# Sample-token products of a hybrid decoder step: the states move through TensorE, and padded k and q columns are the weights

## Chip, core and metric

The kernel runs on one core of one Trainium2 chip. The metric is the device time of one execution in microseconds. TensorE does the matrix products, VectorE (DVE), ScalarE (ACT) and GpSimd (POOL) do the elementwise work, and SyncE (SP) issues most of the transfers.

## What is computed

One layer of a decoder is applied to 512 prompt tokens and to 8 sample tokens. The mixer is a gated delta rule with 8 heads of width 128 beside a pooling group, followed by an output projection and a SwiGLU network. The change concerns the sample tokens alone. For each of the 8 sequences `b` and each of the 8 heads `h` there is a state, a 128 x 128 matrix S, and the recurrent step needs two vectors out of it:

```python
def gated_delta_recurrent(q, k, v, g, beta, S0):
    def step(S, xs):
        q_t, k_t, v_t, g_t, b_t = xs
        S = S * jnp.exp(g_t)[..., None, None]
        kv = jnp.einsum('bhk,bhkv->bhv', k_t, S)
        S = S + jnp.einsum('bhk,bhv->bhkv', k_t, (v_t - kv) * b_t[..., None])
        o = jnp.einsum('bhk,bhkv->bhv', q_t, S)
        return S, o
```

With one token the output can be had from the products of k and q with the incoming state, so the kernel computes k·S and q·S for all 64 pairs (h, b) and does the rest on vectors. The updated states are written much later, in the feed-forward part, from the same inputs.

## The kernel before

**Staging.** The kernel holds the normalised input as two parts `xh` and `xl` of 16 tiles of 128 x 520 (8 sample columns and 512 prompt columns). Every weight granule is loaded as `raw` (L131), cut into `hi` on ScalarE (L135) and `lo` on VectorE (L137), and each product is made of three passes (L168 to L170). One column tile of the input projection is a call of `product`: 16 steps over the depth for the first chunk of columns, and the same for the second chunk three steps behind it.

**The weave.** Small work of the delta rule is written as Python generators and put on tracks of a `Weave`. `product` calls `weave.step()` 16 times for a tile, and each call lets the first task of each track run until its next `yield n`, after which that track rests for n steps. TensorE's instructions are issued in exactly this written order; for the other engines a scheduler orders them by readiness and priority. So a step of the weave is the unit in which small TensorE work is spread between large matmuls.

**The stage of the change.** After the last head's delta rule the pooling tiles run (`pool_tile` for t = 6, 7, 4, 5, 2, 3, 0, 1). Woven into them, on track 0, are `conv_out`, `sample_norms`, eight calls of `sample_product` and `sample_out`; on track 1 is `pool_mix`. After them come the subtraction of L203 over the mixer's first half (`mixa`, its sample columns included, which `sample_out` writes in its L1015) and the splits of the mixer's tiles into `xh` and `xl` (`split`, L194 and L195), which the output projection (L1176 to L1178) reads.

**`sample_norms`** forms k and q of the sample tokens in `kqs`, a tile of 128 x (head, sequence, 2), with k in place 0 and q in place 1 of the last axis. It yields 8, then forms the norms.

**`sample_product(h)`** loads the eight states of a head as two tiles of four (`s0`, L983, through SP's queue, two buffers under the tag `uu`). For each state it issues one f32 matmul with the state as the 128 x 128 weights and the two columns of `kqs` as the moving operand (L986), and yields one step after each. The result is two columns of a PSUM bank. After eight states VectorE copies 16 columns into `smp["kq"]` (L988). A bank comes from `pst()`, which has five.

**`sample_out`** is the chain of vector operations on `kq` (L998 to L1007), a rest of four steps, a matmul with ones (L1010), an inverse root (`rsqrt_wide`) and the write into `mixa` (L1015); it also turns the update vectors and stores them (L1018 to L1021).

**`utfs`** are two tiles of 128 x 1024 that hold the blocks of the triangular inverses for even and odd heads. `delta` reads them (L860, L864, L870, L872), and they are not used after the last head.

Of the kernel before, what the change touches and what calls it, by code (L numbers as in the profile page):

```python
# [17 lines left out]
P = 128  # L18
# [5 lines left out]
H = 8  # L24
# [45 lines left out]
def decoder_kernel(ctx, tc, x_prompt, x_sample, state_delta, state_conv, state_pool, norm_mix, w_in,  # L70
# [4 lines left out]
    te, act, dve, pool, sp = nc.tensor, nc.scalar, nc.vector, nc.gpsimd, nc.sync  # L75
# [12 lines left out]
    def pst():  # L88
        return ps_dn.tile([P, 512], F32, tag="dn", name="dn")


    ident = const.tile([P, P], F32, name="ident")
# [124 lines left out]
    def rsqrt_wide(r, v, t):  # L217

        act.activation(t, v, AF.Sqrt)
        dve.reciprocal(r, t)  # L220
        dve.tensor_tensor(t, v, r, op=ALU.mult)
        dve.tensor_tensor(t, t, r, op=ALU.mult)
        dve.tensor_scalar(t, t, -0.5, 1.5, op0=ALU.mult, op1=ALU.add)
        dve.tensor_tensor(r, r, t, op=ALU.mult)
# [52 lines left out]
    with tc.tile_pool(name="ph0", bufs=2) as ph0, tc.high_priority(offset=10 * AHEAD), tc.manual_schedule():  # L277
# [112 lines left out]
        half = slice(0, D // 2), slice(D // 2, D)  # L390
# [49 lines left out]
        for i in range(17):  # L440
# [48 lines left out]
            ci, j = divmod(i, 8)  # L489
# [31 lines left out]
    with ExitStack() as p1:  # L521
# [4 lines left out]
        def d1tile(tag, shape, name, dtype=F32):  # L526
            return (pre if tag == "ext" else d1).tile(shape, dtype, tag=tag, name=name, bufs=BUFS[tag])

        def scratch(*tags):

            width = {"nb": 1024, "u": 1024}
            tiles = [[d1tile(t, [P, width.get(t, SEQ)], "sc_" + t), 0] for t in tags]

            def take(n):
                for x in tiles:
                    if x[1] + n <= x[0].shape[1]:
                        x[1] += n
                        return x[0][:, x[1] - n:x[1]]
                raise ValueError(n)

            return take
# [99 lines left out]
        kqs = gt.tile([P, H, NB, 2], F32, name="kqs")  # L641
# [69 lines left out]
        utfs = []  # L711
        for i in range(2):
            ut = gt.tile([P, 2, NCH, P], F32, name=f"utf{i}")
# [234 lines left out]
        smp = {}  # L948

        def sample_norms():  # L950
            take = scratch("nb", "u")
            smp["take"] = take
            ys = take(192).rearrange("p (t b) -> p t b", t=24)
            dve.tensor_tensor(ys, ccs.rearrange("p b t -> p t b"),
                              prm[:, 72:96].rearrange("p (t o) -> p t o", o=1).broadcast_to([P, 24, NB]), op=ALU.mult)
            dve.tensor_tensor(ys, ys, scv, op=ALU.add)
            act.activation(kqs[:, :, :, 1], ys[:, 0:8, :], AF.Silu)
            act.activation(kqs[:, :, :, 0], ys[:, 8:16, :], AF.Silu)
            act.activation(vsm, ys[:, 16:24, :], AF.Silu)
            kk, qq = kqs[:, :, :, 0], kqs[:, :, :, 1]  # L960
            sq = take(192).rearrange("p (a h b) -> p a h b", a=3, h=H)
            pool.tensor_tensor(sq[:, 0], kk, kk, op=ALU.mult)
            pool.tensor_tensor(sq[:, 1], qq, qq, op=ALU.mult)
            pool.tensor_tensor(sq[:, 2], kk, qq, op=ALU.mult)
            yield 8
            pn = pst()
            te.matmul(pn[:, 0:192], ones, sq.rearrange("p a h b -> p (a h b)"), start=True, stop=True)
            nv = take(128)
            dve.tensor_scalar(nv, pn[:, 0:128], EPS, None, op0=ALU.add)
            kqd = take(HB)  # L970
            dve.tensor_copy(kqd, pn[:, 128:192])
            rn = take(128)
            rsqrt_wide(rn, nv, take(128))
            smp["rk"], smp["rq"], smp["kqd"] = rn[:, 0:64], rn[:, 64:128], kqd
            dve.tensor_tensor(kns, kk, rn[:, 0:64].rearrange("p (h b) -> p h b", h=H), op=ALU.mult)
            smp["kq"] = take(2 * HB)

        def sample_product(h):

            pk = pst()  # L980
            for hf in range(2):
                s0 = d1tile("uu", [P, 4, P], "s0")
                sp.dma_start(s0, state_delta[0, 4 * hf:4 * hf + 4, h].rearrange("b k v -> k b v"))  # L983
                for j in range(4):
                    b = 4 * hf + j
                    te.matmul(pk[:, 2 * b:2 * b + 2], s0[:, j, :], kqs[:, h, b, :], start=True, stop=True)  # L986
                    yield 1
            dve.tensor_copy(smp["kq"][:, 16 * h:16 * h + 16], pk[:, 0:16])  # L988

        def sample_out():  # L990
            take = smp["take"]
            rk, rq, kqd = smp["rk"], smp["rq"], smp["kqd"]
            pkv = smp["kq"].rearrange("p (n j) -> p n j", j=2)
            vv = vsm.rearrange("p h b -> p (h b)")
            ks, qs, t1, us = take(HB), take(HB), take(HB), take(HB)
            eg = sgb[:, 0].rearrange("p h b -> p (h b)")
            be = sgb[:, 1].rearrange("p h b -> p (h b)")
            dve.tensor_tensor(t1, eg, rk, op=ALU.mult)  # L998
            dve.tensor_tensor(ks, pkv[:, :, 0], t1, op=ALU.mult)
            dve.tensor_tensor(qs, pkv[:, :, 1], eg, op=ALU.mult)  # L1000
            dve.tensor_tensor(us, vv, ks, op=ALU.subtract)
            dve.tensor_tensor(us, us, be, op=ALU.mult)
            dve.tensor_tensor(t1, kqd, rk, op=ALU.mult)
            dve.tensor_tensor(t1, t1, us, op=ALU.mult)
            dve.tensor_tensor(qs, qs, t1, op=ALU.add)
            dve.scalar_tensor_tensor(qs, qs, float(P) ** -0.5, rq, op0=ALU.mult, op1=ALU.mult)
            dve.tensor_tensor(t1, qs, qs, op=ALU.mult)  # L1007
            yield 4
            po = pst()
            te.matmul(po[:, 0:HB], ones, t1, start=True, stop=True)  # L1010
            ov, ro = take(HB), take(HB)
            dve.tensor_scalar(ov, po[:, 0:HB], 1.0 / P, EPS, op0=ALU.mult, op1=ALU.add)
            rsqrt_wide(ro, ov, take(HB))
            dve.tensor_tensor(ro, ro, qs, op=ALU.mult)
            dve.scalar_tensor_tensor(mixa[:, :, 0:NB], ro.rearrange("p (h b) -> p h b", h=H), dnw, mixa[:, :, 0:NB],  # L1015
                                     op0=ALU.mult, op1=ALU.mult)
            pu = pst()
            te.transpose(pu[:HB, 0:P], us, ident)  # L1018
            ur = take(P)[:HB]
            dve.tensor_copy(ur, pu[:HB, 0:P])  # L1020
            sp.dma_start(u_d, ur)  # L1021
            yield 1
# [105 lines left out]
        for b in range(2):  # L1128
# [10 lines left out]
            for h in range(4 * b, 4 * b + 4):  # L1139
                qv_tiles(h)  # L1140
        weave.add(conv_out())
        weave.add(sample_norms())
        for h in range(H):
            weave.add(sample_product(h))
        weave.add(sample_out())
        splits = {}

# [105 lines left out]
    class Pair:  # L1253
# [31 lines left out]
        def take(self):  # L1285
            return pst()[:, :HALF]
# [771 lines left out]
    pt = pst()  # L2058
# [45 lines left out]
```

## Time and profile before

| what | value |
|---|---|
| median of 3 runs | 2156.06 us (2155.36 to 2157.12) |
| the profiled execution, own time | 2156.18 us |
| its span on the core | 2154.4 us |
| granted TensorE clock | 1.0 throughout |
| first and last product (L986) start | 515.2 and 581.0 us |
| states loaded for the products | 16 transfers of 256 KB |

The span runs from the first to the last instruction; the execution's own time is 1.8 us longer. In the rows of the profile, `PE` is a matmul on TensorE and `PEld` its weight load, which overlaps the matmul before it. A row `128*32 128x264` means 128 rows by 32 columns of weights, and 264 moving columns. The lengths of matmuls contain the way through the array and overlap one another, so the price of an instruction in a full stream is read from the distance of starts, not from its length.

### The profile page before, as it was taken

What the parts mean: (1) busy time and instruction counts of PE and PEld (TensorE: products, weight loads), DVE (VectorE), ACT (ScalarE), POOL (GpSimd) and SP (SyncE); (2) the same over time, 40 slices, a digit from 0 to 9 for tenths busy, and PEclk for the clock granted to TensorE, in tenths of its full rate; (3) what the DMA queues carried; (4) which work ended last, traced back from release to release, by engine and by line L of the source; (5) the groups of instructions that cost most, each with busy time, mean ns of one, the idle gap of its engine ahead of it and who ended that gap; (6) DMA issues with size and microseconds to landing.
All of it is one profiled execution on the core that took longest, in us unless ns stands there. A gap on an engine that the chain in (4) does not pass through costs nothing.

```text
span 2154.4 us, 43035 instructions
## 1 busy us (share of the span) xinstructions
PE 2129.6 (99%) x17745; PEld 2121.1 (98%) x17745; DVE 1759.6 (82%) x2635; ACT 929.0 (43%) x1404; POOL 481.9 (22%) x592
## 2 busy tenths in 40 slices
PE   8999999999999999999999999999999999999998
PEld 7999999999999999999999999999999999999998
DVE  7786767666599979888888888888887897887997
ACT  6533452433255454434434434434334444435444
POOL 2112320231012202333233233232113302003100
PEclk9999999999999999999999999999999999999999
DMA  8344434443445534454455455454456746438333
GB/s 282 92 121 110 116 103 117 115 117 98 128 126 166 152 105 124 144 170 144 137 172 147 134 172 147 134 172 133 118 148 195 228 111 205 115 104 247 93 108 119
DMA packets 445826, 305.44 MB, mean 142 GB/s; under 512 B 27836, under 2 KB 424533, under 8 KB 442285
## 3 DMA queue, kind: packets, MB, share of 16 engines
q1 hardware_dynamic: 422733, 219.94, 36.5%
q0 software_dynamic: 21584, 81.95, 12.0%
q8 instruction: 139, 2.28, 0.4%
q10 hardware_dynamic: 1312, 0.80, 0.1%
q14 instruction: 58, 0.48, 0.1%
HBM read 255.66 MB, written 47.63 MB: 141 GB/s over the span
## 4 chain that ended last, share of the span: by engine, by line
PE 85%; DVE 8%; DMA 2%; ACT 2%; issue 2%; POOL 1%; DVEq 0%; ACTq 0%; POOLq 0%; SPq 0%
PE dn L1250 21%; PE dn L1249 21%; PE dn L1251 21%; PE mm L168 6%; PE mm L170 5%; PE mm L169 5%; DVE lo L1243 1%; DVE lo L137 1%; PE dn L870 1%; DMA st<-a_d 1%; DVE raw L1271 1%; POOL st L1803 0%; DVE tm L836 0%; PE dn L986 0%; DVE u L838 0%
## 5 line engine op out<-in xcount | busy, mean ns | idle before, releaser
L1243 DVE TENSOR_TENSOR lo<-raw,hi 128x1024 fp32r<-128x1024 f32 (+1 forms) x422 | 528.6, 1272 | 89.5 <-ACT hi L1242 87.4
L1242 ACT CAST hi<-raw 128x1024 fp32r<-128x1024 f32 (+1 forms) x422 | 427.5, 1027 | 402.9 <-DVE raw L1271 204.2
L168 PE MATMUL mm<-xh,hi 128*128 128x256 f32 (+1 forms) x1280 | 379.5, 297 | 2.6 <-DVE mixa L259 2.6
L169 PE MATMUL mm<-xl,hi 128*128 128x256 f32 (+1 forms) x1280 | 361.6, 283 | 0.9 <-DVE xl L350 0.5
L170 PE MATMUL mm<-xh,lo 128*128 128x256 f32 (+1 forms) x1280 | 361.7, 283 | 0.4 <-DVE lo L137 0.4
L168 PEld LDWEIGHTS mm<-xh,hi 128*128 128x128 f32 x1280 | 241.4, 189 | 3.8 <-DVE mixa L259 3.2
L169 PEld LDWEIGHTS mm<-xl,hi 128*128 128x128 f32 x1280 | 241.7, 189 | 1.7 <-DVE xl L350 1.7
L170 PEld LDWEIGHTS mm<-xh,lo 128*128 128x128 f32 x1280 | 240.9, 188 | 0.6 <-DVE lo L137 0.6
L1271 DVE TENSOR_TENSOR raw<-raw 128x1024 f32<-128x1024 f32 (+1 forms) x130 | 174.6, 1343 | 2.2
L1250 PE MATMUL dn<-b21l,hi 128*128 128x260 f32 x620 | 175.8, 284 | 0.4 <-DVE b21l L1813 0.4
L1251 PE MATMUL dn<-b21h,lo 128*128 128x260 f32 x620 | 175.4, 283 | 0.0
L1249 PE MATMUL dn<-b21h,hi 128*128 128x260 f32 x620 | 174.9, 282 | 0.0
L1251 PE MATMUL dn<-b11h,lo 128*128 128x260 f32 x612 | 173.2, 283 | 1.4 <-DVE lo L1243 1.4
L1250 PE MATMUL dn<-b11l,hi 128*128 128x260 f32 x612 | 173.3, 283 | 0.0
L1249 PE MATMUL dn<-b11h,hi 128*128 128x260 f32 x612 | 172.7, 282 | 0.0
L1435 POOL TENSOR_TENSOR mixa<-mixa 128x520 f32<-128x520 f32 x22 | 51.3, 2330 | 495.5 <-DVE mixa L1429 495.5
L1249 PE MATMUL dn<-T1h,hi 128*128 128x260 f32 x556 | 158.1, 284 | 0.0
L1250 PE MATMUL dn<-T1l,hi 128*128 128x260 f32 x556 | 157.7, 284 | 0.0
L1251 PE MATMUL dn<-T1h,lo 128*128 128x260 f32 x556 | 156.7, 282 | 0.0
L1249 PE MATMUL dn<-B22h,hi 128*128 128x260 f32 x548 | 155.9, 284 | 0.0
L1250 PE MATMUL dn<-B22l,hi 128*128 128x260 f32 x548 | 155.6, 284 | 0.0
L1251 PE MATMUL dn<-B22h,lo 128*128 128x260 f32 x548 | 154.6, 282 | 0.4 <-DVE lo L1243 0.4
(663 smaller groups left out, 6504.0 us busy)
## 6 DMA issues: line engine op xcount, KB each, us to landing
raw<-in_w_gate_up_dram SPq DMA_DIRECT2D x134, 512.0 KB
raw<-in_w_in_dram SPq DMA_DIRECT2D x79, 512.0 KB
a_d<-mixa POOLq DMA_DIRECT2D x22, 1040.0 KB, 5.5
raw<-in_w_down_dram SPq DMA_DIRECT2D x48, 448.0 KB
mixb<-in_w_gate_up_dram SPq DMA_DIRECT2D x41, 512.0 KB
raw<-in_w_out_dram SPq DMA_DIRECT2D x25, 512.0 KB
st<-a_d POOLq DMA_DIRECT2D x49, 260.0 KB, 6.8
raw<-in_w_down_dram SPq DMA_DIRECT2D x24, 512.0 KB
```

What stands on the lines that cost most here:

```text
L137: dve.tensor_tensor(lo[:, r], raw[:, r], hi[:, r].bitcast(F32), op=ALU.subtract)
L168: te.matmul(acc[ci], wh, hi[k][:, c0:c1], start=(k == 0), stop=False)
L169: te.matmul(acc[ci], wh, lo[k][:, c0:c1], start=False, stop=False)
L170: te.matmul(acc[ci], wl, hi[k][:, c0:c1], start=False, stop=(k == len(w) - 1))
L870: te.matmul(yp[0:96, c, j], xt_[:, c, :], udf[:, c, j] if it == 0 else v3(cur)[:, c, j], start=True, stop=True)
L1242: act.copy(hi, raw)
L1243: dve.tensor_tensor(lo, raw, hi.bitcast(F32), op=ALU.subtract)
L1249: te.matmul(acc, wh[:, k, :], xf[:, k, :], start=start and k == 0, stop=False)
L1250: te.matmul(acc, wh[:, k, :], xg[:, k, :], start=False, stop=False)
L1251: te.matmul(acc, wl[:, k, :], xf[:, k, :], start=False, stop=stop and k == wh.shape[1] - 1)
L1271: dve.tensor_tensor(r[name], r[a], r[b], op=op)
L1435: pool.tensor_tensor(q[:, 4:8:2, :], q[:, 1:4:2, :], q[:, 0:2, :], op=ALU.subtract)
```

## The change

The roles of state and vector are exchanged. The states become the moving operand (128 columns), and k and q become weights. For this `sample_norms` builds four areas of 512 columns in the two `utfs` tiles, which are free by then: each is cleared on POOL, and k and q of the 16 states with the same j = b mod 4 are copied in on a diagonal, so that the block of 32 columns with number i holds k and q of its state in columns 2i and 2i + 1 and zeros elsewhere. Four states of one load, j = 0 to 3, then use four groups of 32 columns: the j-th writes the PSUM rows 32j to 32j + 31. All 16 loads add up in the same 128 x 128 block of PSUM: the zeros keep the other rows as they are. The four matmuls of a load are issued together, followed by a rest of four steps, in place of one matmul in each of four steps.

The eight copies out of PSUM go. In their place `sample_out` first copies the block, rests two steps, turns it on TensorE and copies the result into `kq` in the order (i, j, t) that the rest expects.

```diff
@@ -974,22 +974,41 @@
             smp["kq"] = take(2 * HB)
+            smp["cols"] = []
+            kqf = kqs.rearrange("p h b t -> p (h b) t")
+            for ut in utfs:
+                uf = ut.rearrange("p a c j -> p (a c j)")
+                pool.memset(uf, 0.0)
+                for half in range(2):
+                    j, z = len(smp["cols"]), uf[:, 512 * half:512 * half + 512]
+                    src = kqf[:, j:2 * H * 4:4, :]
+                    pool.tensor_copy(z[:, 0:510].rearrange("p (i x) -> p i x", x=34)[:, :, 0:2], src[:, 0:15, :])
+                    pool.tensor_copy(z[:, 510:512], src[:, 15, :])
+                    smp["cols"].append(z)
 
         def sample_product(h):
 
-            pk = pst()
+            if h == 0:
+                smp["pk"] = pst()
             for hf in range(2):
                 s0 = d1tile("uu", [P, 4, P], "s0")
                 sp.dma_start(s0, state_delta[0, 4 * hf:4 * hf + 4, h].rearrange("b k v -> k b v"))
+                i = 2 * h + hf
                 for j in range(4):
-                    b = 4 * hf + j
-                    te.matmul(pk[:, 2 * b:2 * b + 2], s0[:, j, :], kqs[:, h, b, :], start=True, stop=True)
-                    yield 1
-            dve.tensor_copy(smp["kq"][:, 16 * h:16 * h + 16], pk[:, 0:16])
+                    te.matmul(smp["pk"][32 * j:32 * j + 32, 0:P], smp["cols"][j][:, 32 * i:32 * i + 32], s0[:, j, :],
+                              start=(i == 0), stop=(i == 2 * H - 1))
+                yield 4
 
         def sample_out():
             take = smp["take"]
             rk, rq, kqd = smp["rk"], smp["rq"], smp["kqd"]
+            kt = take(P)
+            dve.tensor_copy(kt, smp["pk"][:, 0:P])
+            yield 2
+            pt = pst()
+            te.transpose(pt[:, 0:P], kt, ident)
+            dve.tensor_copy(smp["kq"].rearrange("p (i j t) -> p j i t", j=4, t=2),
+                            pt[:, 0:P].rearrange("p (j i t) -> p j i t", j=4, t=2))
             pkv = smp["kq"].rearrange("p (n j) -> p n j", j=2)
```

## The prediction

> **What bounds the kernel now.** I read the page's busy times first, then its chain of work that ended last, then busy times by stretches around the sample products.
>
> ```profile
> span 2154.4 us, 43035 instructions
> PE 2129.6 (99%) x17745; PEld 2121.1 (98%) x17745; DVE 1759.6 (82%) x2635; ACT 929.0 (43%) x1404; POOL 481.9 (22%) x592
> ...
> PE 85%; DVE 8%; DMA 2%; ACT 2%; issue 2%; POOL 1%; DVEq 0%; ACTq 0%; POOLq 0%; SPq 0%
> ```
> ```profile
> 565.00:581.50 16.50, 16.49 (x139) 16.29 (x140) 7.29 (x17) 2.92 (x4) 0.43 (x3) 1.00 0.52 144
> 581.50:600.00 18.50, 18.50 (x157) 18.50 (x156) 16.10 (x40) 10.73 (x18) 0.21 (x1) 1.00 0.32 89
> 600.00:620.00 20.00, 19.65 (x162) 19.24 (x161) 18.64 (x33) 10.57 (x19) 1.93 (x1) 1.00 0.29 79
> 620.00:640.00 20.00, 19.77 (x164) 19.44 (x162) 19.70 (x31) 11.37 (x20) 3.81 (x7) 1.00 0.55 165
> ```
>
> In the second fence the columns are length, then busy time of PE, PEld, DVE, ACT and POOL, granted clock, DMA share and GB/s. TensorE is busy 99% of the span and holds 85% of the chain that ended last. It sets the time of the products' stage too: it is busy 16.49 of 16.50 us there, VectorE only 7.29. From 581.5 VectorE fills too (16.10 of 18.50, then 18.64 of 20, 19.70 of 20). So TensorE time saved in the products moves everything behind it forward, but only as far as VectorE's first work of the next stage comes forward with it.
>
> **What the products cost now.** The groups of the stretch 515 to 581.5, then TensorE's timeline near their end (start, length, engine, line):
>
> ```profile
> L986 PEld LDWEIGHTS dn<-kqs,s 128*128 128x128 f32 x128 | 19.7, 189 | 0.5 <-DMA s<-in_state_delta_dram 0.5
> L986 PE MATMUL dn<-kqs,s 128*128 128x2 f32 x128 | 18.0, 210 | 0.1
> ```
> ```profile
> 577.72 0.28 PE L170 MATMUL mm<-xh,lo 128*128 128x264 f32 x1
> 577.84 0.28 PE L168 MATMUL mm<-xh,hi 128*128 128x256 f32 x1
> 577.96 0.28 PE L169 MATMUL mm<-xl,hi 128*128 128x256 f32 x1
> 578.07 0.28 PE L170 MATMUL mm<-xh,lo 128*128 128x256 f32 x1
> 578.19 0.28 PE L986 MATMUL dn<-kqs,s 128*128 128x2 f32 x2
> 578.33 0.36 PE L168 MATMUL mm<-xh,hi 128*128 128x264 f32 x1
> 578.54 0.28 PE L169 MATMUL mm<-xl,hi 128*128 128x264 f32 x1
> ```
>
> The 64 calls show as 128 passes: each f32 call is two, each with a weight load of its own. Busy times overlap, so I take the price from starts. From L170 to the next L169 it is 0.24 us without a product (577.72 to 577.96) and 0.47 with one (578.07 to 578.54): **0.23 us a product**, 0.92 for four, 14.7 for 64. What is paid are the loads of 128 columns, with only two columns moving to hide them.
>
> **The new products.** Four calls, eight passes, come together; each loads 32 columns of weights and moves 128 columns of state. The nearest block is eight passes of the same moving size (L618, eight columns of weights). The rows before and behind it, the weight loader's row there, then a block of 32-column weights (L558) in the other number format, and a single small pass that uses 64 rows of the array:
>
> ```profile
> 78.10 1.04 PE L618 MATMUL dn<-triu,sc_g 128*8 128x128 f32 x8
> 79.07 0.40 PE L168 MATMUL mm<-xh,hi 128*128 128x264 f32 x1
> 79.31 0.29 PE L169 MATMUL mm<-xl,hi 128*128 128x264 f32 x1
> ```
> ```profile
> 79.07 0.19 PEld L168 LDWEIGHTS mm<-xh,hi 128*128 128x128 f32 x1 [0.22 <-issue]
> ```
> ```profile
> 50.36 0.28 PE L558 MATMUL dn<-xl,wba 128*32 128x264 f32 x1
> 50.48 0.29 PE L168 MATMUL mm<-xh,hi 128*128 128x264 f32 x1
> ```
> ```profile
> 67.56 0.28 PE L170 MATMUL mm<-xh,lo 128*128 128x256 f32 x1
> 67.77 0.27 PE L670 MATMUL dn<-ident,nt 64*128 64x64 f32 x1
> ```
>
> L618 lasts 1.04 with a last pass of 0.27, so seven starts take 0.77: **0.11 us a pass**. The whole block costs 79.31 - 0.12 - 78.10 = 1.09, which is 8 x 0.11 and 0.21 at its end, where the next weight load was not fetched ahead (0.22 idle). Entering a part of the array costs 0.09 more at L670 (67.56 to 67.77 instead of 0.12). The L558 block leaves at the usual 0.12. So the two edges of a group are between 0 and 0.30; I take 0.30, since L618 has the same number format.
>
> The Trainium skill, "TensorEngine Tiling (Array Packing)", Key Properties, says that a change of tiling mode drains the engine, which speaks against sixteen short groups. L618's 0.21 agrees with it and L558's 0.12 does not; by the rule the edges stay at 0.30, and without it a group would be 0.30 cheaper.
>
> How the eight passes run among themselves no row shows: all of these blocks use one column strip. The bounds are eight after another, 0.88, and four strips at once, two after another, 0.22. I take the middle: passes start in program order, the two of one call share a strip and cannot overlap, but the second of one call and the first of the next sit on different strips and different PSUM rows. That leaves five pass lengths, 0.55. A group is 0.55 + 0.30 = **0.85 us** (bounds 0.22 and 1.18), and sixteen give 16 x (0.85 - 0.92) = **-1.1 us** (bounds -11.2 and +4.2).
>
> **States and their loads.**
>
> ```profile
> PEld dn L986 <- DMA s<-in_state_delta_dram: 0.5, 2, 0.3
> ```
> ```profile
> 540.10 4.62 DMA s<-in_state_delta_dram
> ```
>
> Two products wait for a state now, 0.5 us in all. A step of the weave is six passes, 0.72 us, and 0.95 with a product. A buffer came free at the fourth of its steps and its successor's successor was due five steps on; now it is released at the first, eight steps ahead, two groups of four steps (4 x 0.72 + 0.85 = 3.7 us each). The 4.62 us load fits in 6.6, and demand hardly rises (3.7 us a state against 3.8). **-0.5** (0 if SP's queue, which holds weight loads too, eats the gain). The products now hold one of the five PSUM banks from first to last; before, one was held by each head in turn, so the rest has four as before: 0.
>
> **Columns on POOL.** Two clears and eight small copies are added ahead of the first product. Their tile is read last by the step of L872 that starts at 489.07. A clear, POOL's queue around this time, and that last reader with the first product:
>
> ```profile
> L714 POOL MEMSET utf<- x2: 955/1094/1233, 46.9 to 47.8; 128x1024 f32 x2
> ```
> ```profile
> 483.64 0.74 POOL L964 TENSOR_TENSOR sc_nb<-kqs 128x64 f32<-128x64 f32 x1
> ...
> 513.07 1.12 POOL L1068 COPY pcp<-pe 128x15 f32<-128x15 f32 x1
> 515.31 2.59 POOL L769 DMA_DIRECT2D mixb<-tok_d  x4 [1.11 <-DMA tok_d<-bt]
> ...
> 525.17 0.21 POOL L1068 COPY pcp<-pe 128x15 f32<-128x15 f32 x1 [7.15 <-DVE pe L259]
> ```
> ```profile
> 489.07 0.29 DVE L872 SCALAR_TENSOR_TENSOR uu<-dn,utf 96x128 f32<-96x128 f32 x1 [1.37 <-PE dn L870]
> ...
> 515.20 0.28 PE L986 MATMUL dn<-kqs,s 128*128 128x2 f32 x2
> ```
>
> Two clears take 2.2 us. For a copy the near rows are 0.21 and 1.12 (L1068), so eight are 1.6 to 9. The first product starts at 515.2, so between 489.4 and there 25.8 us cover the 3.8 to 11.2. Behind the clears in POOL's queue stand small powers and DMAs of the last head; nothing on TensorE waits for those here. The squares of the same step (L964) were drawn forward to 483.64 although written far later, so I expect the same of these copies. **0**; the price without cover is a rival below.
>
> **The turn at the end.** Eight copies of VectorE (L988) go; they lie in its idle time: 0. Two copies, one transpose and two more steps of the weave come in. The transpose's price, from one of the same moving size, by starts: 606.61 to 606.96 instead of 0.24, so **+0.1** (bounds: 0, if hidden, to 0.2).
>
> ```profile
> 606.61 0.28 PE L1178 MATMUL mm<-xh,lo 128*128 128x260 f32 x1
> ...
> 606.96 0.28 PE L1177 MATMUL mm<-xl,hi 128*128 128x260 f32 x1
> ```
>
> The two steps matter through VectorE. The chain of work, in order of time, leaves TensorE at 587.94 and stays on VectorE to 609.67:
>
> ```profile
> 587.94 0.42 DVE pe L259
> 588.91 0.25 DVE mixa L1015
> 589.18 2.39 DVE mixa L203 x2
> ```
> ```profile
> 609.67 0.39 PE L169 MATMUL dn<-dl,hi 128*128 128x264 f32 x1 [0.35 <-DVE dl L195]
> ```
>
> L1015 writes the sample columns of `mixa`, and the long subtraction L203 needs them. In the new order L1015 stands two steps later against TensorE's work, 2 x 0.72 = 1.44 us. Behind it on VectorE wait L203 and all splits into `xl`, and for these TensorE at 609.67. How much of the 1.44 comes through: all of it, if VectorE has nothing to put in its place; nothing, if the 1.2 us split of a weight granule and an eviction move ahead of it. I take half, **+0.7** (bounds 0 and 1.4).
>
> **Sum.** -1.1 - 0.5 + 0.1 + 0.7 = -0.8 us against the profiled execution's own 2156.18 (span 2154.4); the median of the runs shown is 2156.06, 0.12 lower, within their spread. Forecast **2155.4 us**.
>
> **The rivals.** All take the terms other than the group as above, together +0.3.
>
> *Four strips at once.* The group is two passes, 0.22 + 0.30 = 0.52: 16 x (0.52 - 0.92) = -6.4, so 2150.1. For it: strips and PSUM rows are disjoint. Against it: the two passes of one call stand next to each other in the program, and passes start in order in every row. The Trainium skill, "TensorE: Matmul & The Clock Gate", Part 3, reports matmuls on different column strips starting about 4 ns apart and 2.38 times the speed for three; by it this rival holds. No row here shows two strips at work.
>
> *Edges cost nothing.* As forecast, but leaving like L558: the group is 0.55, 16 x (0.55 - 0.92) = -5.9, so 2150.6. For it L558, with just 32 columns; against it L618, in the number format of the products. With both of these rivals true, 0.22 a group, it is 2145.3.
>
> *The strips do not run side by side* (slower). In effect the change then does not do what its words say. Eight passes after another and both edges, 0.88 + 0.30 = 1.18: 16 x (1.18 - 0.92) = +4.2, so 2160.7; at L618's own 1.09 it is 2159.2. It makes the kernel slower as a whole from a group of 0.90 on, and by over 0.2% from 1.17. For it: it is what L618's row says as it stands, where 128 moving columns cost a pass as much as a load of 128 weights did. Against it: L618 has a single strip.
>
> *Columns late* (slower). If POOL's order puts clears and copies behind L769, which ends at 517.9, they are ready at 521.7 to 529.1, and TensorE, which takes its work in written order, stands from 515.2: 6.5 to 14 us, some 2162 to 2170. For it: POOL's queue is in order and L769 waits on a DMA. Against it: L964 was drawn forward past the same DMAs.
>
> **How the numbers follow.** Forecast 0.43; four strips at once 0.18; edges free 0.12; strips one after another 0.22; columns late 0.05. I give the forecast most because it follows from order and from disjoint strips alone, and the serial case next because it is the only one with a row. A measurement of this kernel can tell 0.2%, 4.3 us, from no change. Faster by more: the second case, most of the third, a sliver of the first, 0.29. Slower by more: of the serial case the part at 1.17 and above, 0.13, the late columns, 0.05, a sliver of the first, 0.01, together 0.19. The rest, 0.52, is no change. The range runs from 2149.5, which holds the two faster rivals but not both at once, to 2161.5, the serial case with part of VectorE's 1.4; what is left out is the late columns and both faster rivals together. The forecast's own range, with edges of at least L618's 0.21 (a group of 0.76) and VectorE's and the load's bounds, is 2153.1 to 2156.7.
>
> **What would show it.** In TensorE's timeline, from the L170 ahead of a group to the L169 behind it, less 0.24: 0.85 is right, 0.52 or 0.55 is a faster rival, about 1.1 the serial one. Starts inside a group tell which: pairs 0.11 apart with the next call beside the second of the last (forecast), all four together, or eight at 0.11. The weight loader's row behind a group shows 0.2 of idle or none. POOL's clears should lie between 489 and 510 and TensorE should have no gap at 515; a gap there is the last rival. Waits for the state's DMA should be gone. From `sample_out`'s copy to L1015 the distance should grow by about 1.4, and TensorE's wait at L169 (0.35 us now) by up to that. The forecast is wrong if a group lies outside 0.6 to 1.1 or if VectorE's stretch to 609 is moved by something else.

## The result and the profile after

| | median | runs | profiled execution | its span |
|---|---|---|---|---|
| before | 2156.15 us (2155.30 to 2157.97) | 15 | 2156.18 us | 2154.4 us |
| changed | 2151.22 us (2150.07 to 2153.17) | 15 | 2151.82 us | 2150.1 us |

The ratio is 0.9977, with a 95% interval from 0.9969 to 0.9985. The changed kernel is 4.9 us (0.23%) faster, where 0.8 us had been forecast. Its page:

```profile
span 2150.1 us, 43041 instructions
PE 2123.7 (99%) x17746; PEld 2110.5 (98%) x17746; DVE 1757.6 (82%) x2629; ACT 929.3 (43%) x1404; POOL 490.9 (23%) x602
...
PE 85%; DVE 8%; DMA 2%; issue 2%; ACT 1%; POOL 1%; DVEq 0%; SPq 0%; ACTq 0%; POOLq 0%
```

TensorE still bounds the kernel, and it is busy 5.9 us less (2129.6 before). The work went out of the products. Their two groups in the stretch from 515 to 580 us (busy time, mean ns of one, idle time before them):

```profile
L998 PE MATMUL dn<-s,utf 128*32 128x128 f32 x128 | 6.8, 285 | 0.0
L998 PEld LDWEIGHTS dn<-s,utf 128*32 128x32 f32 x128 | 2.5, 108 | 2.2 <-issue 0.2
```

There are again 128 passes, but they keep TensorE busy for 6.8 us where L986 took 18.0, and their weight loads take 2.5 us where they took 19.7. No wait for a state's transfer is left on these rows (0.5 us before). The second group of four calls in TensorE's timeline, then the weight loader's rows there:

```profile
520.23 0.28 PE L170 MATMUL mm<-xh,lo 128*128 128x256 f32 x1
520.44 0.42 PE L998 MATMUL dn<-s,utf 128*32 128x128 f32 x8
520.79 0.39 PE L168 MATMUL mm<-xh,hi 128*128 128x264 f32 x1
521.02 0.29 PE L169 MATMUL mm<-xl,hi 128*128 128x264 f32 x1
```
```profile
520.43 0.16 PEld L998 LDWEIGHTS dn<-s,utf 128*32 128x32 f32 x8
520.79 0.19 PEld L168 LDWEIGHTS mm<-xh,hi 128*128 128x128 f32 x1 [0.20 <-issue]
```

A strip is one of the four groups of 32 columns, with its 32 PSUM rows. From L170 to L169 it is 0.79 us; less the 0.24 of a stream without a product, a group costs **0.55**. The fifteen groups that could be measured this way have a median of 0.553. How the eight passes run inside it shows when the same group is cut into stretches (length, busy time of PE with the number of passes in flight, the same of PEld, granted clock, DMA share, GB/s):

```profile
520.40:520.50 0.10, 0.06 (x4) 0.07 (x8) 1.00 1.22 318
520.50:520.65 0.15, 0.15 (x8) 0.09 (x8) 1.00 1.22 301
520.65:521.00 0.35, 0.21 (x8) 0.00 (x0) 1.00 1.26 211
```

Four passes start within the first 0.06 us. In the records of the trace the eight start at 0, 0.007, 0.013, 0.020 and then at 0.133, 0.140, 0.147, 0.153 us. The records do not say which pass belongs to which call. Together with the runs on one strip and on pairs below, they read as two *turns*: first the first passes of all four calls, side by side on the four strips, and then the four second passes.

Not all of the gain arrives. The next table compares matmul starts, counted from the first matmul of the kernel, with those of the profile of before (plus is later); the last column is the last stretch of the kernel.

| | at 470 us | 500 | 582 | 624 | 2100 |
|---|---|---|---|---|---|
| changed kernel | +0.51 | +1.90 | -4.17 | -2.99 | -4.17 |

The products bring 6.1 us (500 to 582), but 1.4 us are lost ahead of them (470 to 500) and 1.2 us behind them (582 to 624). Another -1.2 us comes after 624; its cause stays open, and at least part of it may be scatter, since the profiles with unchanged products move by 0 to -0.8 us there. The times in the head are those of the profile of before, so the added transpose, 0.1 us at 578.92 of the changed kernel's own time, lies behind the mark of 582. The rest of the loss behind the products is on VectorE. The same stretches as before (length, then busy time of PE, PEld, DVE, ACT and POOL), the chain of work in order of time, and TensorE's matmul that waits at its end:

```profile
565.00:581.50 16.50, 16.50 (x150) 15.50 (x149) 8.09 (x23) 3.35 (x4) 0.32 (x2) 1.00 0.39 110
581.50:600.00 18.50, 18.16 (x152) 17.96 (x152) 17.59 (x36) 12.46 (x21) 0.21 (x1) 1.00 0.30 88
600.00:620.00 20.00, 19.22 (x157) 18.77 (x156) 17.97 (x33) 12.33 (x22) 1.23 (x1) 1.00 0.35 96
620.00:640.00 20.00, 18.89 (x157) 18.68 (x157) 19.97 (x30) 9.12 (x13) 4.80 (x8) 1.00 0.54 163
```
```profile
579.35 0.30 DVE sc_nb L1010
...
580.74 0.24 DVE sc_u L1024
581.14 1.22 DVE lo L137
582.36 0.14 DVE sc_u L1026
582.55 0.45 PE dn L1029 x2
...
585.70 0.29 DVE mixa L1034
586.02 2.39 DVE mixa L203 x2
```
```profile
606.26 0.39 PE L169 MATMUL dn<-dl,hi 128*128 128x264 f32 x1 [0.78 <-DVE dl L195]
```

TensorE has more gaps after the products than before: it is busy 18.16 of 18.50 us and 19.22 of 20, where it was 18.50 and 19.65. A 1.22 us split of a weight granule (L137) stands in the middle of the sample chain, TensorE waits 0.3 us for the operand of L1029 from that chain, and the wait at L169 has grown from 0.35 to 0.78 us. VectorE's L203 starts at 586.02, only 3.2 us earlier than before (589.18).

### The profile page after: what moved, and what is told of

Its sections match the earlier page's. It is cut to its first block, busy times and chain, and to the rows that moved or that the text cites. A ratio compares the mean times of both kernels' runs of the same rounds, so it can differ in the third digit from the quotient of the medians.

```text
span 2150.1 us, 43041 instructions
## 1 busy us (share of the span) xinstructions
PE 2123.7 (99%) x17746; PEld 2110.5 (98%) x17746; DVE 1757.6 (82%) x2629; ACT 929.3 (43%) x1404; POOL 490.9 (23%) x602
## 4 chain that ended last, share of the span: by engine, by line
PE 85%; DVE 8%; DMA 2%; issue 2%; ACT 1%; POOL 1%; DVEq 0%; SPq 0%; ACTq 0%; POOLq 0%
PE dn L1269 21%; PE dn L1268 21%; PE dn L1270 21%; PE mm L168 5%; PE mm L170 5%; PE mm L169 5%; DVE lo L1262 1%; DVE lo L137 1%; PE dn L870 1%; DMA st<-a_d 1%; DMA qk<-tok_d 1%; PE mm L1268 1%; PE mm L1269 0%; DVE raw L1290 0%; PE mm L1270 0%
## 5 line engine op out<-in xcount | busy, mean ns | idle before, releaser
L1262 DVE TENSOR_TENSOR lo<-raw,hi 128x1024 fp32r<-128x1024 f32 (+1 forms) x422 | 530.6, 1277 | 87.0 <-ACT hi L1261 85.5
L168 PE MATMUL mm<-xh,hi 128*128 128x256 f32 (+1 forms) x1280 | 376.4, 294 | 3.1 <-DVE mixa L259 3.1
L169 PE MATMUL mm<-xl,hi 128*128 128x256 f32 (+1 forms) x1280 | 361.6, 283 | 0.9 <-DVE xl L350 0.7
L170 PE MATMUL mm<-xh,lo 128*128 128x256 f32 (+1 forms) x1280 | 361.7, 283 | 0.4 <-DVE lo L137 0.4
L168 PEld LDWEIGHTS mm<-xh,hi 128*128 128x128 f32 x1280 | 241.2, 188 | 7.1 <-DVE mixa L259 3.8
L169 PEld LDWEIGHTS mm<-xl,hi 128*128 128x128 f32 x1280 | 241.6, 189 | 1.7 <-DVE xl L350 1.7
L170 PEld LDWEIGHTS mm<-xh,lo 128*128 128x128 f32 x1280 | 240.9, 188 | 0.6 <-DVE lo L137 0.6
```

What stands on the lines that cost most here:

```text
L168: te.matmul(acc[ci], wh, hi[k][:, c0:c1], start=(k == 0), stop=False)
L169: te.matmul(acc[ci], wh, lo[k][:, c0:c1], start=False, stop=False)
L170: te.matmul(acc[ci], wl, hi[k][:, c0:c1], start=False, stop=(k == len(w) - 1))
L1262: dve.tensor_tensor(lo, raw, hi.bitcast(F32), op=ALU.subtract)
```

## The experiments

Three questions: do the strips carry the gain, what does a group cost in parts, and where are the 1.4 and the 1.2 us lost? All diffs are against the changed kernel unless said otherwise. The columns of the table that closes this section were read in each run as above.

### One strip instead of four

The four calls of a load all write PSUM rows 0 to 31, into four places of 128 columns. The weights, states and number of calls are the same; the one transpose at the end becomes four.

```diff
-                    te.matmul(smp["pk"][32 * j:32 * j + 32, 0:P], smp["cols"][j][:, 32 * i:32 * i + 32], s0[:, j, :],
-                              start=(i == 0), stop=(i == 2 * H - 1))
+                    te.matmul(smp["pk"][0:32, P * j:P * j + P], smp["cols"][j][:, 32 * i:32 * i + 32], s0[:, j, :],
+                              start=(i == 0 and j == 0), stop=(i == 2 * H - 1 and j == 3))
...
-            te.transpose(pt[:, 0:P], kt, ident)
+            for j in range(4):
+                te.transpose(pt[:, 32 * j:32 * j + 32], kt[:, P * j:P * j + P], ident[:32, :32])
```

> The changed kernel, but all four calls of a group write the same 32 PSUM rows (one column strip, four places side by side in the bank), and the turn is four small transposes. Theory, the strips working side by side pay: the eight passes then run one after another as in L618, a group costs 8 x 0.11 + 0.30 = 1.18 us instead of the 0.55 measured, 16 x 0.63 = +10 us on the changed kernel's 2151.2, about 2161; starts inside a group 0.11 apart. Rival, the gain comes from moving the state alone (32 columns of weights load faster than 128): the group stays near 0.55 and the time near 2151.

Measured: 2162.33 us, ratio 1.0025 (1.0014 to 1.0035), slower than before. The group in its timeline, and cut into stretches:

```profile
520.25 0.28 PE L170 MATMUL mm<-xh,lo 128*128 128x256 f32 x1
520.46 1.06 PE L998 MATMUL dn<-s,utf 128*32 128x128 f32 x8
521.45 0.39 PE L168 MATMUL mm<-xh,hi 128*128 128x264 f32 x1
521.67 0.29 PE L169 MATMUL mm<-xl,hi 128*128 128x264 f32 x1
```
```profile
520.40:520.50 0.10, 0.04 (x1) 0.05 (x2) 1.00 1.61 446
520.50:520.65 0.15, 0.15 (x2) 0.15 (x3) 1.00 0.85 205
```

A group is 521.67 - 520.25 - 0.24 = 1.18 us (median 1.187), and only one pass starts in the first 0.1 us where four did. The passes start 0.11 us apart, as in L618's row in the prediction. So smaller weights alone do not pay: with the same 32 columns but a single strip the change loses. The four strips carry the whole gain.

### Groups of two and of eight calls

Two calls at a time, with a rest of two steps between them; and eight calls of a head at a time, with the second load in a buffer of another tag.

```diff
-                yield 4
+                    if j % 2:
+                        yield 2
```
```diff
-                s0 = d1tile("uu", [P, 4, P], "s0")
+                s0 = d1tile(("uu", "bt")[hf], [P, 4, P], "s0")
...
-                yield 4
+            yield 8
```

> The changed kernel with groups of two calls every two steps instead of four every four. Theory, a group pays its two edges (0.30) and two pass lengths, however many strips are used: 32 groups at about 0.5 us, 16 to 17 us instead of 8.8, about 2159. Rival, the price is per call (0.14 each): 64 x 0.14 as now, about 2151. Starts inside a group: 0, 0.007, 0.13, 0.14 if the first passes of all calls go before the second passes; four within 0.02 if the array simply takes four loads at a time.

> The changed kernel with both states tiles of a head used in one group of eight calls every eight steps; the second tile has buffers of its own (tag bt), so that loads stay one head ahead. Theory, edges are paid per group: 0.55 + 2 more pass lengths of 0.13 = 0.82 a group, 8 x 0.82 = 6.5 us instead of 8.8, about 2149. Rival, price per call: about 2151. A wait of a group for its states would show as TensorE idle in front of L998.

Measured: 2160.52 us for pairs, ratio 1.0017 (1.0008 to 1.0027), and 2148.87 us for eights, ratio 0.9962 (0.9947 to 0.9977). A pair, then a group of eight:

```profile
520.40 0.28 PE L170 MATMUL mm<-xh,lo 128*128 128x256 f32 x1
520.61 0.41 PE L998 MATMUL dn<-s,utf 128*32 128x128 f32 x4
...
521.18 0.28 PE L169 MATMUL mm<-xl,hi 128*128 128x264 f32 x1
```
```profile
522.25 0.28 PE L170 MATMUL mm<-xh,lo 128*128 128x256 f32 x1
522.46 0.64 PE L998 MATMUL dn<-s,utf 128*32 128x128 f32 x16
...
523.26 0.28 PE L169 MATMUL mm<-xl,hi 128*128 128x256 f32 x1
```

A pair costs 0.54 us, as much as four calls, and eight cost 0.77. In the records the four passes of a pair start at 0, 0.007, 0.133 and 0.140 us: its second passes wait although two strips are free, so the turns do not come from a limit of four passes at a time. The price hangs on the number of turns, not on the number of passes: two turns 0.55, four turns 0.77, and the eight single-strip passes, eight turns, 1.19. That is **0.34 us for each group and 0.107 for each turn**. In pairs, fours and on one strip alike the first pass starts 0.21 us behind L170, the next L168 starts 0.20 us behind the last pass, and the weight loader is idle for 0.20 us. The products of before (L986) are f32 calls too, but on the full width: they start 0.12 us behind L170 and leave no idle time. So the number format alone does not make the edges. Pairs pay the 0.34 thirty-two times, which makes them slower than the kernel before.

### The end of the products

The rest behind the last group is cut from four steps to one, so that `sample_out` begins three steps earlier.

```diff
-                yield 4
+                yield 4 if i < 2 * H - 1 else 1
```

> The changed kernel, but after the last group the rest is one step instead of four, so that sample_out begins three steps earlier and L1034 (the write into mixa) stands one step earlier against TensorE's work than before the change. Theory, VectorE's stretch behind that write costs TensorE about 1 us in the changed kernel (its lead falls from 4.2 to 3.2 us between 585 and 640): that comes back, about 2150.2, and the lead stays at 4 us behind 640. Rival, the stretch waits on something else (weights, the eviction): 2151.2 as now.

Measured: 2151.08 us, ratio 0.9972 (0.9962 to 0.9983). The changed kernel itself was run once more beside the next two, for its scatter.

> The changed kernel once more, beside the two versions below on one chip. Its first profile had lost 1.4 us at 480 us, ahead of every changed instruction, where the read of tok_d landed later. If that is a scatter of transfers between executions, this profile shows less of it and TensorE's first product again stands within 1 us of where the other versions have it; if the cleared columns on POOL cause it, the 1.4 us return. Ratio to before 0.9977 as measured first.

Measured: 2151.54 us, ratio 0.9976 (0.9966 to 0.9986). In the early version the lead stays as it was from 582 to 624 us (-0.03 instead of +1.18 and +1.22 in the two profiles of the changed kernel), and the wait behind VectorE is as short as before:

```profile
604.18 0.39 PE L169 MATMUL dn<-dl,hi 128*128 128x264 f32 x1 [0.36 <-DVE dl L195]
```

So 1.1 of the 1.2 us are the lateness of `sample_out` against VectorE's work; the other 0.1 is the added transpose, which in this version lies ahead of the mark of 582. In the time of the kernel they cannot be told: the intervals of the ratios overlap, and from 700 to 1000 us this version gives 0.6 us back to waits for the split of weights (L1262).

Groups of eight and the early end together:

> Groups of eight calls and sample_out three steps earlier together. Theory: a group costs 0.34 + 0.107 us for each two calls' pass lengths in turn (fitted on 0.54, 0.55, 0.77 and 1.19), so 8 x 0.77 = 6.1 instead of 8.8 us (-2.7), and VectorE's 1.2 us come back: 3.9 below the changed kernel, ratio to before 0.9959. Rival, the two do not add, since other waits on VectorE take the second gain: -2.7, 0.9964.

Measured: 2148.43 us, ratio 0.9961 (0.9948 to 0.9974). The loss from 582 to 624 is again nearly gone (+0.19), and the time is that of the groups of eight.

Sixteen calls, two heads at a time, with a last rest of 13 steps:

> Groups of sixteen calls (two heads, four state tiles under the tags uu, uu, bt and tq, without a second set) every sixteen steps, sample_out at the same step as in the run with eight. Theory, edges per group: 0.34 + 8 x 0.107 = 1.20 us, 4 x 1.20 = 4.8 instead of 8.8 us (-4.0), and 1.2 from VectorE: 5.2 below the changed kernel, ratio 0.9953. Rival, the states come late: 1 MB has 16 x 0.72 = 11.5 us to land behind a group, beside weight loads; if it does not, TensorE stands in front of L998-type matmuls by some us and the ratio is above that of groups of eight.

Measured: 2149.68 us, ratio 0.9965 (0.9952 to 0.9978). A group costs 1.21 us, as the rule has it (0.34 + 8 x 0.107 = 1.20). The gain is given back at one place in the products' stage:

```profile
527.74 0.19 PEld L168 LDWEIGHTS mm<-xh,hi 128*128 128x128 f32 x1 [1.97 <-issue]
```

The list of waits (total, times, longest) names the eviction of a pooling tile out of PSUM:

```profile
PE mm L168 <- DVE pcs L259: 1.8, 1, 1.8
```

Why VectorE is late there was not followed up. Larger groups than eight gained nothing here.

### The loss ahead of the products

All eight profiles so far with the new columns had matmuls at 500 us later than the one profile of before, by 0.5 to 1.9 us. Either POOL's new work causes that, or the profile of before was a lucky one. Two more profiles of the kernel before, and the kernel before with the columns built but not used:

> The kernel before, once more. Theory A, the changed column code costs time ahead of the products (POOL's clear at 457 us moves its later transfers, and the read of qk from tok_d lands later: waits of 2.41 to 3.39 us in the seven changed profiles against 2.03 us): the wait of L923 is again 2.0 +- 0.2 us, and matmuls at 500 us start within 0.3 us of the first profile of before. Rival B, transfers scatter and the first profile of before had a lucky one: the wait is anywhere from 2.0 to 3.4 us, and the matmuls at 500 us start up to 1.5 us later than in the first profile. Time 2156.5 +- 1.

> The kernel before with the two clears and eight copies of the zero-padded columns added on POOL and nothing that reads them; the products and all behind them as before. Theory A: the wait of L923 is 2.4 us or more, matmuls at 500 us start 0.8 to 1.5 us later than in before, and the kernel takes 0.5 to 1.5 us longer (ratio 1.0003 to 1.0007). Rival B: as before, ratio 1.0000 +- 0.0008, the lead at 500 us not larger than that of the other profile of before, except for 0.4 to 0.6 us where TensorE now waits for POOL in the last head (L870, 1.15 us after POOL L986, against 0.63 us of issue in before).

> The kernel before, a third profile, for the scatter of the wait of L923 and of the matmul starts at 500 us. Theory A: 2.0 +- 0.2 us and within 0.3 us of the first profile. Rival B: somewhere from 2.0 to 3.4 us, and up to 1.5 us later.

Measured: between 470 and 500 us the second and third profile of before move by +0.55 and +0.30 us against the first, the columns by +1.38. The whole times (2155.74, 2157.34 and 2157.22 us; ratio of the columns 1.0003, 0.9994 to 1.0013) cannot tell. The profile can. POOL's rows in the kernel with the columns, then ScalarE's first reader of `qk`:

```profile
457.69 0.96 POOL L981 MEMSET utf<- 128x1024 f32 x1 [1.31 <-DVE uu L872]
...
470.20 0.62 POOL L754 DMA_DIRECT2D tok_d<-bt  x1 [5.56 <-DVE bt L753]
473.28 2.19 POOL L759 DMA_DIRECT2D qk<-tok_d  x4 [2.45 <-DMA tok_d<-bt]
```
```profile
480.08 0.31 ACT L923 ACTIVATE junk<-qk 128x128 f32<-128x128 f32 x1 [3.37 <-DMA qk<-tok_d]
```

The first clear is not at 489 us, where the second of the two tiles falls free, but at 457.69, ahead of the last head's way through memory (q and k written by L754 and read back by L759). To see whether this clear does it, ScalarE was given the two clears, first in the kernel with unused columns and then in the groups of eight with the early end:

```diff
-                pool.memset(uf, 0.0)
+                act.activation(uf, uf, AF.Copy, scale=0.0)
```

> As e9_columns_only, but ScalarE clears the two halves (multiplying them by 0) in place of POOL; the copies stay on POOL; nothing reads them. Theory A, POOL's 0.96 us clear ahead of its transfers of the last head is what moves them: the write L754 lands again 2.0 to 2.1 us after its issue (2.45 with the clear on POOL, 2.04 to 2.05 in three profiles of before), the read of qk is issued before the state read, the wait of L923 is 2.0 to 2.6 us, the step of the matmul starts between 471 and 486 us is 0 to 0.6 us instead of 1.38. Rival B, the place of the clear does not matter: 2.4 to 2.5 us, a wait of 2.9 to 3.4 us, a step of 0.8 to 1.4 us. Ratio by A 1.0000 +- 0.0008, by B 1.0004 +- 0.0008.

> e6_eight_early (groups of eight calls, the last rest 5) with the clears on ScalarE. By theory A the 0.8 to 1.1 us of the last head come back: ratio 0.9956 +- 0.001 against the kernel before (2147.3 us where that takes 2156.8), the lead at 500 us 0 to +0.6 and at 582 -8 us; by B as e6: 0.9961 +- 0.001, the lead at 500 us +0.8 to +1.9.

POOL's transfers and their reader with the clear on ScalarE (columns unused):

```profile
469.92 0.62 POOL L754 DMA_DIRECT2D tok_d<-bt  x1 [5.56 <-DVE bt L753]
472.58 0.57 POOL L759 DMA_DIRECT2D qk<-tok_d  x1 [2.03 <-DMA tok_d<-bt]
473.31 1.64 POOL L759 DMA_DIRECT2D qk<-tok_d  x3 [0.16 <-issue]
```
```profile
472.74 0.37 SPq L994 DMA_DIRECT2D s<-in_state_delta_dram  x1
```
```profile
478.81 0.31 ACT L923 ACTIVATE junk<-qk 128x128 f32<-128x128 f32 x1 [2.37 <-DMA qk<-tok_d]
```

With the clear on POOL the first read of `qk` waits 2.35 to 2.53 us for the write, in nine profiles of nine, and with none there 2.03 to 2.05, in five of five. In these rows the first read of `qk` goes out at 472.58, ahead of the first state's 256 KB on SP's queue (472.74); in the changed kernel it is the other way round, the state's transfer at 473.11 and the reads from 473.43. The same holds in all: the state's transfer goes first in the nine profiles with the clear on POOL, the read in the five without. The wait of L923 falls from 3.37 to 2.37 us, and the step from 470 to 500 us from +1.38 to +0.38, within that of the profiles of before (0 to +0.55). With the clear on POOL that step is 0.88 to 1.39 us in eight of nine profiles (0.40 in the early end's), without it 0 to 0.55 in all five: the clear costs about 1 us. Why a clear that is over 11 us before the write makes it land 0.3 to 0.5 us later is open.

In whole times: 2157.42 us, ratio 1.0001 (0.9992 to 1.0010), for the unused columns with the clear on ScalarE, and **2148.18 us, ratio 0.9959** (0.9945 to 0.9972), for groups of eight with the early end and that clear. This is the fastest version here, but its interval overlaps that of the other groups of eight.

All runs by stretches of their profile (us of matmul starts against the first profile of before, minus is time won). In the versions with the early end the transpose's 0.1 us falls into the stretch to 582, in the other ones with new products behind it:

| kernel | 470 to 500 | 500 to 582 | 582 to 624 | ratio |
|---|---|---|---|---|
| changed | +1.39 | -6.07 | +1.18 | 0.9977 |
| changed, again | +1.38 | -6.07 | +1.22 | 0.9976 |
| one strip | +0.88 | +4.02 | +1.61 | 1.0025 |
| pairs | +1.32 | +2.41 | +1.16 | 1.0017 |
| eights | +1.09 | -8.79 | +1.22 | 0.9962 |
| early end | +0.40 | -5.97 | -0.03 | 0.9972 |
| eights, early end | +1.36 | -8.67 | +0.19 | 0.9961 |
| sixteens, early end | +0.98 | -7.92 | +0.16 | 0.9965 |
| before, second and third | +0.55, +0.30 | -0.07, -0.27 | 0.00, -0.02 | |
| unused columns, clear on POOL | +1.38 | +0.06 | 0.00 | 1.0003 |
| unused columns, clear on ScalarE | +0.38 | -0.02 | 0.00 | 1.0001 |
| eights, early end, clear on ScalarE | +0.26 | -8.67 | +0.18 | 0.9959 |

## Why the prediction was right or wrong

The time, 2151.2 us, lies inside the range, but the forecast's mechanism was wrong, and the runs show the mechanism of the rival *four strips at once* (2150.1). By its own sign the forecast is wrong: a group was to cost 0.6 to 1.1 us and costs 0.553, and the time lies outside the forecast's own 2153.1 to 2156.7. The wider range holds it because it was drawn to hold the rivals, and because two losses that the prediction had too small, the clear's and VectorE's, moved the time back towards it. The gain of 0.23% is just past the 0.2% that the prediction said could be told, a case that it gave 0.29.

- **The step that failed** is "passes start in program order, the two of one call share a strip and cannot overlap", with five pass lengths a group. The trace shows two turns, the first passes of all four calls and then the second ones, 0.553 us a group where 0.85 was forecast and 0.52 stood in the rival. By the prediction's 0.92 for four products, sixteen groups so give 16 x (0.553 - 0.92) = -5.9 us, not -1.1. The premise (one strip holds one pass at a time) stood; the order did not. The traces do not show whether the passes stand in this order in the program or TensorE takes them so. The bound of two passes after another, 0.22, stood in the prediction, and it is what two turns cost.
- **The rule that spoke for this rival.** The prediction cited the Trainium skill, "TensorE: Matmul & The Clock Gate", Part 3: matmuls on different column strips start about 4 ns apart. Here they start 7 ns apart, which comes to the same for this kernel. It was the only source for two strips at work, and it was given a chance of 0.18.
- **The edges, 0.30**, were right: 0.34 a group. That they cost nothing, as behind L558, is excluded: the weight load behind a group comes after 0.20 us of idle. The rule in the Trainium skill, "TensorEngine Tiling (Array Packing)", Key Properties, that a change of mode drains the engine agrees with these rows: pairs pay the 0.34 twice as often and lose. L558, whose weights have 32 columns too, still shows no such price; why it does not is open.
- **Strips one after another** is excluded for the change and is what one strip alone does: 1.187 us a group (1.18 forecast), and +4.02 us over the stage, against +4.2 for the products and -0.5 for the loads.
- **State loads, -0.5**: the waits for the transfer are gone. Two products of before had waited for a state; measured as the others were, they cost 0.39 and 0.27 us more than the median, 0.7 in all. That median is 0.223 us and not 0.23, so four products are 0.89 us and not 0.92, and the groups bring 5.4 us and not 5.9. This closes the sum: the 64 products of before add up to 15.0 us and the sixteen groups to 8.9, a difference of 6.1 where the stage won 6.07. Pairs add up to 17.5 and eights to 6.2, which gives +2.5 and -8.8 where the stage shows +2.41 and -8.79.
- **Columns, 0**: they are drawn forward and ready in time, as forecast (POOL's last copy ends at 493.8 us, the first product starts at 517.0), and TensorE has no gap at the first product. What was missed is a clear drawn forward past a transfer on which TensorE's chain depends, about +1 us. The prediction took both clears to be bound by the last reader at 489 us, but the other of the two tiles is free from 457 us, and "nothing on TensorE waits" was asked only of what stood behind 489 us.
- **The turn at the end, +0.1** (the added transpose, not a turn of the strips): from 578.92 to 579.27 us, 0.11 above the usual 0.24. Right.
- **VectorE, +0.7, bounds 0 and 1.4**: the mechanism was right and the size was nearer the upper bound, 1.1 us. The split L137 did not move ahead of the chain, as the lower bound supposed, but into it.

The terms as measured, -5.4 - 0.7 + 0.1 + 1.1 + 1.0 = -3.9 us, agree with the two profiled executions (-4.4) within the scatter of single profiles, which for the kernel before is 1.6 us between the three. The medians differ by 4.9 us, with an interval from 3.2 to 6.7, which holds the sum.

## What to carry to other kernels

Small products whose weight load has nothing to hide behind become cheap when they share TensorE by column strips, but only in groups large enough for a price of about a third of a microsecond each; in these runs such a group is priced in turns of the strips, not in passes. Where a trace shows a block only with one strip, it says nothing of four, and a middle between the bounds is a guess that deserves no more chance than the bound with a reason behind it. Before you call work on an idle engine free, look at what stands behind it in that engine's queue, from the moment at which its operands fall free and not from the place at which the program writes it: here a clear that was long over went with a later transfer, and only a run with the clear on another engine showed it.

## What the runs showed of the hardware

- Four f32 calls on four column strips run as two turns. Passes in one turn start 0.007 us apart, the second turn 0.133 us after the first, later turns 0.11 us apart (groups of eight and sixteen). Eight passes on one strip are 0.11 us apart too.
- A group of 32-column calls between full-width matmuls costs 0.34 us beside its turns of 0.107, whether it holds two, four, eight or sixteen calls (0.54, 0.55, 0.77 and 1.21 us).
- A clear of 0.96 us on POOL, over long before POOL's next transfer, goes with a landing of that transfer 0.3 to 0.5 us later: the next read waits 2.35 to 2.53 us in each of nine profiles with it, and 2.03 to 2.05 in each of the five without.
